# A two-layer hybrid decoder on one core: the weight sums of paired up-projection columns move from VectorE to accumulating transfers that GpSimd issues, and three more pairs of columns are formed

## The chip, the core and the metric

The kernel runs on one core of a Trainium2 chip. The metric is the time of one execution in microseconds, as the device reports it; lower is better. The engines are called as the profile calls them: PE is TensorE, ACT is ScalarE, DVE is VectorE, POOL is GpSimd, SP is SyncE, which here only issues DMAs.

## The reference

The input is 512 tokens of width 1024, with 16 learned tokens put ahead, 528 in all. Each of two layers is a mixer (projections, retention and gated linear attention heads, an output projection) and a gated MLP, each between two RMS norms with a residual. The change touches the MLP's up projection, 1024 to 2 x 2816:

```
def _conv_ffn(h, ffn_up, ffn_conv_w, ffn_conv_b, ffn_down):
    length = h.shape[1]
    u = h @ ffn_up
    up = jnp.pad(u, ((0, 0), (CONV_W - 1, 0), (0, 0)))
    conv = ffn_conv_b + sum(up[:, i:i + length] * ffn_conv_w[i] for i in range(CONV_W))
    a, g = jnp.split(conv, 2, axis=-1)
    return (jax.nn.gelu(a, approximate=True) * g) @ ffn_down
```

Everything is float32 at the kernel's boundary.

## The kernel before, in words

Activations lie transposed: features on the 128 partitions, tokens along the free dimension. Each float32 operand of a large product is split into two float16 parts, a high one and a low one, and a product is three matmuls: high x high, high x low, low x high (lines 534 to 536; in pairs, line 1296). For a weight, ACT makes the high part (a scaled copy) and DVE the low part (scaled weight less the high part). Both go to a buffer called a unit, of which there are 10; PE reads units only.

Weights come in by SP's loads, into float32 stage cells (`st`) of 4 KB per partition: 8 cells in the first layer, 5 in the second. The plan makes one list of blocks for the whole program, and each block is loaded and converted in the order of that list, up to 10 blocks ahead of the one that PE uses. So how far the weights run ahead is set by the cells, by the units, and by how fast ACT and DVE come to them. From the middle of the first mixer on, a scheduler orders the instructions of each engine; loads and, here, some others keep the order of the program.

The up projection has 22 columns per layer. A column here is 128 features of the first half (`upa`) with the 128 features of the gate half that go with them (`upg`). After it come the convolution (ACT one step, DVE two, line 1342), the gelu, the product of the halves and its split into two float16 parts. A plain column is two blocks of 1024 x 128 weights and eight products of 3 matmuls, in two parts by tokens (232 and 296; 218 and 296 in the second layer).

Some columns are instead made as pairs, by a product scheme of the Strassen kind (`paired`, line 1283 on). The weights of the column are a 2 x 2 matrix of quarters, w11, w12 (gate half), w21, w22 (lower 512 rows), and the tokens are cut into two halves of 264. Seven products of 4 x 3 matmuls over 264 tokens take the place of eight. For that, sums of the activations are formed once per layer and sums of the weights for each pair. A pair stands in the list as four pieces (`PairPiece`): piece 0 holds w11 and w22; piece 1 holds w11 + w12 and w12 + w22; piece 2 holds w11 + w12 + w22 and w21; piece 3 holds the sum of all four. Before the change DVE forms the sums in place in two stage cells (line 215), four steps per pair, each between the conversions that read the old value and those that read the new one. PE accumulates the products in PSUM banks (`pp`), from the same three that the plain products use; ACT copies intermediate results out (`part`, line 1304, and `u`, line 1326) and DVE combines them (line 1308).

In the first layer nine columns are pairs: 9, 11, 13, 14, 15, 17, 19, 20, 21; in the second two: 8 and 10. GpSimd takes part in the norms, in rotary steps and in roots, and issues two DMAs late in the program (line 1468).

Of the kernel before, what the change touches and what calls it, by code (L numbers as in the profile page):

```python
# [9 lines left out]
F32 = mybir.dt.float32  # L10
U8 = mybir.dt.uint8
AF = mybir.ActivationFunctionType
ALU = mybir.AluOpType

P = 128
# [30 lines left out]
SLOTS = 41  # L46
AHEAD = 10
# [21 lines left out]
PAIRED = {0: (9, 11, 13, 14, 15, 17, 19, 20, 21), 1: (8, 10)}  # L69
HK2 = KD // 2  # L70
# [117 lines left out]
class PairPiece:  # L188
# [10 lines left out]

    def fetch(self):  # L200
        if self.unit is not None:
            return
        kern, nc = self.kern, self.kern.nc
        if self.step == 0:
            self.st = []
            for half in (((0, 0), (1, 1)), ((0, 1), (1, 0))):
                st = cell(kern.stage, [P, 2, HK2, P], F32, *kern.stage_of(self.layer))
                for i, (a, b) in enumerate(half):
                    load = nc.sync.dma_start(st[:, i], self.src[512 * a : 512 * (a + 1), self.cols[b] : self.cols[b] + P].rearrange("(k p) c -> p k c", p=P))
                    kern.tc.keep_in_program_order(load)  # L210
                self.st += [st[:, 0], st[:, 1]]
                if len(self.st) == 2:
                    self.both = st
        w = self.first.st
        add = lambda to, x: nc.vector.tensor_tensor(out=w[to], in0=w[to], in1=w[x], op=ALU.add)
        if self.step == 0:
            parts = [(slice(0, 2), self.both)]
        elif self.step == 1:
            add(0, 2)
            add(2, 1)  # L220
            parts = [(0, w[0]), (1, w[2])]
        elif self.step == 2:
            add(0, 1)
            parts = [(0, w[0]), (1, w[3])]
        else:
            add(0, 3)
            parts = [(0, w[0])]
        u = self.unit = cell(kern.wpool, [P, 2, 2, HK2, P], F16, "unit", "unit", UNITS)
        for i, st in parts:
            self.hi = nc.scalar.activation(u[:, 0, i], st, AF.Copy, scale=SW)  # L230
            nc.vector.scalar_tensor_tensor(out=u[:, 1, i], in0=st, scalar=SW, in1=u[:, 0, i], op0=ALU.mult, op1=ALU.subtract)


class Kern:
# [495 lines left out]
    def plan(self):  # L730
        a = self.a
# [7 lines left out]
        for l in range(DEPTH):  # L739
# [4 lines left out]
            for i in range(KF):  # L744
                if i in PAIRED[l]:
                    first = None
                    for q in range(4):
                        self.key[l, "pair", i, q] = len(self.blocks)
                        self.blocks.append(PairPiece(self, l, a["ffn_up"][l], (P * i, DFF + P * i), q, first))
                        first = first or self.blocks[-1]  # L750
                    continue
# [889 lines left out]
```

## Time and profile before

| | |
|---|---|
| median of three runs | 1195.14 us (1195.05 to 1195.2) |
| profiled execution, its own time | 1195.35 us |
| its span in the profile | 1193.5 us |
| PE, DVE, ACT, POOL busy | 1183.8, 879.8, 682.5, 184.1 us |
| HBM read | 120.24 MB |
| loads of 256 KB from the up projection's weights (pairs) | 44 |
| loads of 512 KB from the up projection's weights (plain columns) | 66 |

The span is divided into stages, by PE's products: first mixer and output projection to 263 us, first up projection to 495, down projection from 490 to 603, then the second mixer and output projection to 854, the second up projection to 1085, and the last down projection to the end. The pairs of the first layer are used between 362 and 495 us, those of the second between 939 and 974. Busy time on an engine says nothing by itself; what counts is who waits for whom where PE would otherwise go on. In rows of the timeline the columns are start, length, engine, line and operation, output and inputs, and the count of like instructions that follow each other; in rows that group instructions, the busy time, the mean length of one, and the idle time before them with what ended it.

### The profile page before, as it was taken

Reading aid. Unit: us, or ns where it says so; the run is one execution under the profiler, and the core shown is the slowest. Engines: PE = TensorE matmul, PEld = TensorE weight load, DVE = VectorE, ACT = ScalarE, POOL = GpSimd, SP = SyncE. Lnnn points to the kernel's source line nnn. Section 1 sums busy time; section 2 is a strip of 40 time slices with the busy share of each in tenths; the row PEclk is TensorE's granted clock in tenths of the full one; section 3 lists DMA queues with packets and bytes.
Section 4 is the critical chain, followed back from the end, with each engine's and each line's share of the span. In section 5 each row is a group of like instructions: output and inputs, shape, how many; then the busy total and the mean of one; then the engine's idle time right before and its main releaser. Section 6 shows DMA issues by size and latency. Waiting matters only on the chain.

```text
span 1193.5 us, 26242 instructions
## 1 busy us (share of the span) xinstructions
PE 1183.8 (99%) x10910; PEld 998.4 (84%) x10910; DVE 879.8 (74%) x1539; ACT 682.5 (57%) x1351; POOL 184.1 (15%) x213
## 2 busy tenths in 40 slices
PE   8999999999999999999999999999999999999998
PEld 8888889989888888988888888899888888886445
DVE  6687855368998999833565968553799998797687
ACT  6685444564876676633346854445657676664452
POOL 2132311263000000000331414012620000000000
PEclk9999999999999999999999999999999999999999
DMA  8933131122613242642235132211422453206371
GB/s 224 276 108 96 54 90 54 37 65 78 177 36 89 77 119 74 184 112 77 80 99 142 55 89 72 72 54 37 124 71 72 125 164 110 99 1 225 117 250 71
DMA packets 207066, 124.02 MB, mean 104 GB/s; under 512 B 6928, under 2 KB 194500, under 8 KB 206948
## 3 DMA queue, kind: packets, MB, share of 16 engines
q1 hardware_dynamic: 206356, 121.37, 34.8%
q8 instruction: 85, 1.39, 0.5%
q0 software_dynamic: 160, 0.52, 0.1%
q10 hardware_dynamic: 432, 0.46, 0.1%
q14 instruction: 33, 0.27, 0.1%
HBM read 120.24 MB, written 2.10 MB: 103 GB/s over the span
## 4 chain that ended last, share of the span: by engine, by line
PE 87%; DVE 3%; issue 1%; ACT 1%; POOL 1%; POOLq 0%; DVEq 0%; ACTq 0%
PE pu L535 10%; PE pu L534 10%; PE pu L536 10%; PE pl L1480 8%; PE pp L1296 7%; PE pj L534 6%; PE pj L535 6%; PE pj L536 6%; PE pd L534 3%; PE pd L536 3%; PE pd L535 3%; PE po L534 2%; PE po L536 2%; PE po L535 2%; PE o L851 1%
## 5 line engine op out<-in xcount | busy, mean ns | idle before, releaser
L536 PE MATMUL pu<-every,unit 128*128 128x296 f16 (+2 forms) x1056 | 289.1, 274 | 0.0
L535 PE MATMUL pu<-every,unit 128*128 128x296 f16 (+2 forms) x1056 | 289.0, 274 | 0.0
L534 PE MATMUL pu<-every,unit 128*128 128x296 f16 (+2 forms) x1056 | 288.7, 274 | 0.0
L534 PEld LDWEIGHTS <-unit 128*128 128x128 f16 x2508 | 246.1, 98 | 35.4
L536 PEld LDWEIGHTS <-unit 128*128 128x128 f16 x2508 | 245.3, 98 | 36.2
L535 PEld LDWEIGHTS <-unit 128*128 128x128 f16 x2508 | 245.3, 98 | 35.5
L534 PE MATMUL pj<-every,unit 128*128 128x296 f16 (+2 forms) x888 | 244.3, 275 | 0.0
L535 PE MATMUL pj<-every,unit 128*128 128x296 f16 (+2 forms) x888 | 244.3, 275 | 0.0
L536 PE MATMUL pj<-every,unit 128*128 128x296 f16 (+2 forms) x888 | 244.2, 275 | 0.0
L131 DVE SCALAR_TENSOR_TENSOR unit<-st,unit 128x1024 f16<-128x1024 f32 (+2 forms) x161 | 196.7, 1229 | 43.5 <-ACT unit L123 43.3
L123 ACT ACTIVATE unit<-st 128x1024 f16<-128x1024 f32 x159 | 164.9, 1041 | 44.9 <-PE pd L536 20.4
L459 POOL TENSOR_TENSOR every<-every 128x5 f32<-128x5 f32 (+6 forms) x31 | 37.3, 1205 | 556.3 <-DVE every L458 463.2
L1296 PEld LDWEIGHTS <-unit 128*128 128x128 f16 x924 | 90.4, 98 | 14.0 <-issue 0.4
L492 DVE TENSOR_TENSOR acc<-acc,sq 128x296 f32<-128x296 f32 (+2 forms) x60 | 32.3, 541 | 75.0 <-ACT sq L490 69.5
L536 PE MATMUL pd<-av,unit 128*128 128x232 f16 (+1 forms) x308 | 84.7, 276 | 0.0
L535 PE MATMUL pd<-av,unit 128*128 128x232 f16 (+1 forms) x308 | 84.6, 276 | 0.0
L534 PE MATMUL pd<-av,unit 128*128 128x296 f16 (+1 forms) x308 | 84.4, 276 | 0.0
L1353 ACT ACTIVATE u<-pu 128x296 f32<-128x296 f32 (+2 forms) x132 | 49.8, 378 | 49.2 <-PE pu L536 48.0
L1480 PE MATMUL pl<-unit,fk 128*128 128x512 f16 x330 | 71.4, 379 | 0.0
L1342 DVE SCALAR_TENSOR_TENSOR cg<-u,every,cg 128x527 f32<-128x527 f32 (+1 forms) x88 | 66.3, 754 | 4.7 <-ACT cg L1337 4.3
L536 PE MATMUL po<-merged,unit 128*128 128x296 f16 (+2 forms) x256 | 69.7, 274 | 0.0
L535 PE MATMUL po<-merged,unit 128*128 128x296 f16 (+2 forms) x256 | 69.7, 274 | 0.0
(279 smaller groups left out, 1938.9 us busy)
## 6 DMA issues: line engine op xcount, KB each, us to landing
st<-in_ffn_up SPq DMA_DIRECT2D x66, 512.0 KB, 4.8
st<-in_w_in SPq DMA_DIRECT2D x56, 512.0 KB, 4.1
st<-in_ffn_down SPq DMA_DIRECT2D x46, 512.0 KB, 4.9
st<-in_ffn_up SPq DMA_DIRECT2D x44, 256.0 KB, 3.4
st<-in_w_out SPq DMA_DIRECT2D x16, 512.0 KB, 4.1
st<-in_ffn_down SPq DMA_DIRECT2D x8, 384.0 KB, 6.7
out<-yo SPq DMA_DIRECT2D x7, 256.0 KB, 2.0
w<-in_ffn_down SPq DMA_DIRECT2D x3, 512.0 KB, 5.1
```

Source lines behind the costliest of these rows:

```text
L123: self.hi = self.kern.nc.scalar.activation(self.unit[:, 0], self.st, AF.Copy, scale=SW)
L131: self.last = self.kern.nc.vector.scalar_tensor_tensor(out=out, in0=x, scalar=SW, in1=high, op0=ALU.mult, op1=ALU.subtract)
L459: nc.gpsimd.tensor_tensor(out=r[:w, :n], in0=t[:w, :n], in1=self.mhalf[:w, :n], op=ALU.pow)
L492: self.summed = eng.tensor_tensor(out=acc[:, :n], in0=acc[:, :n], in1=sq[:, :n], op=ALU.add)
L534: nc.tensor.matmul(ps[:, :n], w[:, 0, kk, :], x[:, 0, n0:n1], start=first, stop=False)
L535: nc.tensor.matmul(ps[:, :n], w[:, 0, kk, :], x[:, 1, n0:n1], start=False, stop=False)
L536: nc.tensor.matmul(ps[:, :n], w[:, 1, kk, :], x[:, 0, n0:n1], start=False, stop=last)
L851: nc.tensor.matmul(o[:, i, :], intra(i + 1), vn(i + 1), start=i == 0, stop=i == 0, skip_group_check=i > 0)
L1296: mm = lambda p, q, **kw: nc.tensor.matmul(ps, u[:, p, k, :], x[k][:, q], skip_group_check=more, **kw)
L1342: nc.vector.scalar_tensor_tensor(out=to, in0=u[:, max(lo, d) - d : L - d], scalar=self.cvec[:, ci(i) : ci(i) + 1], in1=to, op0=ALU.mult, o ...
L1353: nc.scalar.activation(u[:, n0:n1], ps[:, : n1 - n0], AF.Copy, scale=IXW)
L1480: mm = lambda x, w, **kw: nc.tensor.matmul(ps[:, cols], x, w[:, cols], skip_group_check=more, **kw)
```

## The change

Three things change, all in how pairs are prepared and which columns are pairs.

First, the weight sums are no longer made by DVE. Each pair gets a third cell, with two more quarters: `wa` and `wd`, both loaded as w11. SP now loads six quarters of 256 KB per pair in a given order instead of four. GpSimd then issues five transfers that add what they read to what lies in their destination: with piece 0, w12 from HBM into wa, w22 into w12, w21 into wd, and the new w12 into wd; with piece 1, the new w12 into w11. The first reads HBM, the other four copy inside SBUF. They keep the program's order in GpSimd's queue. Piece 1 is made from wa and w12, piece 2 from w11 and w21, piece 3 from wd. The third cell comes from a ring of four cells of its own in the first layer (`wx`) and from the five stage cells in the second.

Second, piece 0 of each pair changes places in the list with the block ahead of it, so that its loads and sums are asked for one block earlier; the order in which PE uses the blocks is looked up by key and follows.

Third, eleven columns of the first layer are pairs (10, 16 and 18 are new, 15 is plain) and three of the second (12 is new). 

```diff
+WX = 4
-PAIRED = {0: (9, 11, 13, 14, 15, 17, 19, 20, 21), 1: (8, 10)}
+PAIRED = {0: (9, 10, 11, 13, 14, 16, 17, 18, 19, 20, 21), 1: (8, 10, 12)}
...
+    def load(self):
+        kern, nc = self.kern, self.kern.nc
+        more = (kern.keep, "wx", "wx", WX) if self.layer == 0 else (kern.stage, *kern.stage_of(self.layer))
+        cells = [cell(pool, [P, 2, HK2, P], F32, *tag) for pool, *tag in [(kern.stage, *kern.stage_of(self.layer))] * 2 + [more]]
+        quarter = lambda a, b: self.src[512 * a : 512 * (a + 1), self.cols[b] : self.cols[b] + P].rearrange("(k p) c -> p k c", p=P)
+        order = ((0, 0, 0, 0), (0, 1, 1, 1), (1, 0, 0, 1), (2, 0, 0, 0), (1, 1, 1, 0), (2, 1, 0, 0))
+        for c, i, a, b in order:
+            load = nc.sync.dma_start(cells[c][:, i], quarter(a, b))
+            kern.tc.keep_in_program_order(load)
+        (w11, w22), (w12, w21), (wa, wd) = ((c[:, 0], c[:, 1]) for c in cells)
+        self.parts = [(slice(0, 2), cells[0])], [(0, wa), (1, w12)], [(0, w11), (1, w21)], [(0, wd)]
+        self.adds = [(wa, quarter(0, 1)), (w12, w22), (wd, w21), (wd, w12)], [(w11, w12)], [], []
+
+    def sums(self, step):
+        for to, x in self.adds[step]:
+            add = self.kern.nc.gpsimd.dma_start(out=to, in_=x, accum_op=ALU.add)
+            self.kern.tc.keep_in_program_order(add)
...
         if self.step == 0:
...
+            self.load()
+        self.first.sums(self.step)
+        parts = self.first.parts[self.step]
...
-        add = lambda to, x: nc.vector.tensor_tensor(out=w[to], in0=w[to], in1=w[x], op=ALU.add)
-        if self.step == 0:
-            parts = [(slice(0, 2), self.both)]
-        elif self.step == 1:
-            add(0, 2)
-            add(2, 1)
-            parts = [(0, w[0]), (1, w[2])]
-        elif self.step == 2:
-            add(0, 1)
-            parts = [(0, w[0]), (1, w[3])]
-        else:
-            add(0, 3)
-            parts = [(0, w[0])]
...
+                    n = self.key[l, "pair", i, 0]
+                    self.blocks[n - 1 : n + 1] = self.blocks[n - 1 : n + 1][::-1]
+                    self.key = {k: {n - 1: n, n: n - 1}.get(v, v) for k, v in self.key.items()}
```

On POOL, before, the norms of the first layer's second token part (`acc`, the residual in `every`, `tmp`) are followed at once by those of the down projection:

```order
L514 TENSOR_TENSOR every_79<-every_79,tmp_4094 128x296
L514 TENSOR_TENSOR every_79<-every_79,tmp_4100 128x296
L459 TENSOR_TENSOR every_79<-every_79 99x3
L459 TENSOR_TENSOR every_79<-every_79 116x2
L514 TENSOR_TENSOR every_79<-every_79,tmp_8015 128x232
```

After, the sums of all eleven pairs stand between them; here the end of the first norms and the sums of columns 9 and 10 (`st_4288` holds w11 and w22 of column 9, `st_4289` w12 and w21, `wx_4290` wa and wd):

```order
L513 TENSOR_TENSOR every_79<-every_79,tmp_4100 128x296
L458 TENSOR_TENSOR every_79<-every_79 99x3
L216 DMA wx_4290<-in_ffn_up 128x4x128
L216 DMA st_4289<-st_4288 128x512
L216 DMA wx_4290<-st_4289 128x512 x2
L216 DMA st_4288<-st_4289 128x512
L216 DMA wx_4868<-in_ffn_up 128x4x128
L216 DMA st_4867<-st_4866 128x512
L216 DMA wx_4868<-st_4867 128x512 x2
L216 DMA st_4866<-st_4867 128x512
```

In each pair the fifth sum, into the first cell, stands ahead of the next pair's first four.

On ACT, before, the conversions of the pair of column 15 (`st_5684`, `st_5687`) stand among the copies out of PSUM (`part`) of the pairs of columns 13 and 14, `pp_5786` and the two after it, and `pp_5919`:

```order
L1304 ACTIVATE part_5807<-pp_5786 128x264
L230 ACTIVATE unit_5790<-st_5684 128x512
L1393 ACTIVATE ca_5772<-ca_5772 128x528
L1304 ACTIVATE part_5827<-pp_5787 128x264
L230 ACTIVATE unit_5790<-st_5687 128x512
L1304 ACTIVATE part_5845<-pp_5786 128x264
L230 ACTIVATE unit_5810<-st_5687 128x512
L230 ACTIVATE unit_5810<-st_5684 128x512
L463 ACTIVATE av_4523<-cg_5773 128x528
L1304 ACTIVATE part_5938<-pp_5919 128x264
L230 ACTIVATE unit_5830<-st_5684 128x512
```

After, the pair of column 16 is converted there (`st_5718` w11 and w22, `st_5719` w12 and w21, `wx_5720` wa and wd), among the copies of the pairs of columns 13 (`pp_5827`) and 14 (`pp_5970`, `pp_5971`):

```order
L1306 ACTIVATE part_5880<-pp_5827 128x264
L229 ACTIVATE unit_5731<-st_5718 128x1024
L124 ACTIVATE unit_5845<-st_5843 128x1024
L229 ACTIVATE unit_5863<-wx_5720 128x512
L229 ACTIVATE unit_5863<-st_5719 128x512
L229 ACTIVATE unit_5922<-st_5719 128x512
L1306 ACTIVATE part_5984<-pp_5970 128x264
L1306 ACTIVATE part_6001<-pp_5971 128x264
L229 ACTIVATE unit_5922<-st_5718 128x512
L1306 ACTIVATE part_6021<-pp_5970 128x264
L229 ACTIVATE unit_5940<-st_5927 128x1024
```

The conversion of w11 for piece 2 (`unit_5922<-st_5718`) now stands between the copies of the second and the third product of column 14, and reads a value that the sum on POOL must have written since the conversion of `unit_5731`; in the rows of before the sums were DVE's, and wa and wd did not exist.

More of the change, by code (lines that the diff above doesn't have):

```diff
@@ L204, in fetch @@
         if self.step == 0:
[L205 to L215, printed above, removed]
-        if self.step == 0:
-            parts = [(slice(0, 2), self.both)]
-        elif self.step == 1:
-            add(0, 2)
-            add(2, 1)
-            parts = [(0, w[0]), (1, w[2])]
-        elif self.step == 2:
-            add(0, 1)
-            parts = [(0, w[0]), (1, w[3])]
-        else:
-            add(0, 3)
-            parts = [(0, w[0])]
+            self.load()
+        self.first.sums(self.step)
+        parts = self.first.parts[self.step]
         u = self.unit = cell(kern.wpool, [P, 2, 2, HK2, P], F16, "unit", "unit", UNITS)
```

## The prediction

> **What bounds the kernel now.** I read the page first (busy times and the chain that ended last), then the waits of PE, then the two up projections, where the pairs are.
>
> ```profile
> PE 1183.8 (99%) x10910; PEld 998.4 (84%) x10910; DVE 879.8 (74%) x1539; ACT 682.5 (57%) x1351; POOL 184.1 (15%) x213
> ...
> PE 87%; DVE 3%; issue 1%; ACT 1%; POOL 1%; POOLq 0%; DVEq 0%; ACTq 0%
> ```
>
> ```profile
> PE pts L606 <- DVE ndg L714: 1.3, 1, 1.3
> ...
> PE pp L1296 <- ACT part L1304: 0.2, 1, 0.2
> ```
>
> PE is busy for 99% of the span, and its longest waits are 1.3 us in all. In the pairs it waited once, 0.2 us for a copy by ACT. So time is what PE has to stream, plus any stall that is newly made. The stretch of the first up projection with most of its pairs, by engine:
>
> ```profile
> core 0: us, PE busy (x) PEld busy (x) DVE busy (x) ACT busy (x) POOL busy (x), PEclk, DMA share, GB/s
> 362.00:485.00 123.00, 122.80 (x1092) 106.63 (x1090) 115.09 (x177) 85.39 (x153) 0.00 (x0) 1.00 0.37 104
> ```
>
> PE is full at a granted clock of 1.00, DVE is busy 94%, GpSimd not at all, the DMA engines 37%. The waits of this stretch, and DVE's and ACT's groups by form:
>
> ```profile
> ACT unit L230 <- DVE st L215: 12.8, 13, 3.1
> ```
>
> ```profile
> L231 DVE SCALAR_TENSOR_TENSOR unit<-st,unit 128x512 f16<-128x512 f32 x36 | 24.0, 685 | 3.3 <-ACT unit L230 3.1
> L215 DVE TENSOR_TENSOR st<-st 128x512 f32<-128x512 f32 x29 | 19.9, 685 | 0.2
> L131 DVE SCALAR_TENSOR_TENSOR unit<-st,unit 128x1024 f16<-128x1024 f32 x10 | 12.1, 1222 | 1.0 <-ACT unit L123 1.0
> L1308 DVE SCALAR_TENSOR_TENSOR u<-pp,part 128x264 f32<-128x264 f32 x24 | 9.9, 424 | 1.9 <-ACT unit L123 1.1 <-ACT unit L230 0.8
> ...
> L231 DVE SCALAR_TENSOR_TENSOR unit<-st,unit 128x1024 f16<-128x1024 f32 x7 | 8.5, 1216 | 0.0
> ```
>
> ```profile
> L230 ACT ACTIVATE unit<-st 128x512 f16<-128x512 f32 x36 | 21.6, 623 | 13.1 <-DVE st L215 12.3 <-PE pu L536 0.6
> ...
> L1304 ACT ACTIVATE part<-pp 128x264 f32<-128x264 f32 x25 | 9.6, 383 | 8.3 <-PE pp L1296 8.2
> ...
> L230 ACT ACTIVATE unit<-st 128x1024 f16<-128x1024 f32 x7 | 7.3, 1047 | 0.3 <-PE pp L1296 0.3
> ```
>
> ACT already waits for the weight sums on DVE, up to 3.1 us at a time, and PE hardly feels it: units are ready well ahead.
>
> **PE's own saving.** Starts of matmuls that open a column without a pair, in the first and in the second up projection, and pieces of the chain for the pairs:
>
> ```profile
> 340.67 0.26 PE L534 MATMUL pu<-every,unit 128*128 128x232 f16 x1
> ...
> 351.47 0.26 PE L534 MATMUL pu<-every,unit 128*128 128x232 f16 x1
> ```
>
> ```profile
> 907.86 0.26 PE L534 MATMUL pu<-every,unit 128*128 128x218 f16 x1
> ...
> 918.38 0.26 PE L534 MATMUL pu<-every,unit 128*128 128x218 f16 x1
> ```
>
> ```profile
> 374.60 1.35 PE pp L1296 x12
> ...
> 402.93 27.00 PE pp L1296 x240
> ```
>
> A column without a pair costs 351.47 - 340.67 = 10.80 us, in the second projection 918.38 - 907.86 = 10.52. A pair is 7 products of 1.35, 9.45 us (240 matmuls in 27.00 give the same 112.5 ns each). Two more pairs in the first projection and one in the second: 2 x 1.35 + 1.07 = 3.77 us less for PE. Nothing hides this, since PE is the path.
>
> **DVE and ACT.** Removed: 44 sums of 0.685. Added per new pair on DVE: 5 x 0.685 + 1.216 + 3 x 0.424 against 2 x 1.222, so 3.5 us. In the stretch above, 29 sums go (19.9) and two pairs come (7.0): about 102 of 120 us instead of 115 of 123. ACT gains 5 x 0.623 + 1.05 - 2 x 1.05, about 2.1 per pair: 89 of 120. PE did not wait for DVE here, so the relief is worth nothing by itself; it is room for the pairs. What is late next, if anything, are the sums as transfers.
>
> **What the sums cost as transfers.** The trace has no accumulating transfer, so I bound it. Loads of the same 256 KB by SP, and the only transfers that GpSimd issues, also 256 KB, amid a run of SP loads:
>
> ```profile
> L209 SPq DMA_DIRECT2D st<-in_ffn_up x44: 367/498/1904, 301.2 to 922.2; - x44
> ...
> DMA to landing us min/median/max: 2.9/3.4/5.3
> ```
>
> ```profile
> L1468 POOL DMA_DIRECT2D every<-in_post_ffn_norm x2: 554/648/742, 1084.6 to 1085.3; - x2
> ...
> DMA to landing us min/median/max: 6.9/7.2/7.5
> ```
>
> ```profile
> 1082.48 0.37 SPq L153 DMA_DIRECT2D every<-in_ffn_down  x1
> ...
> 1085.24 8.84 SPq L153 DMA_DIRECT2D st<-in_ffn_down  x6
> ```
>
> So a sum takes 2.9 to 7.5 us from issue to landing. By kind it is nearest to the GpSimd row, but that one stood beside a run of SP loads, and the stretch of the pairs moves data only 37% of the time now. I take 5.5, an estimate between the medians 3.4 and 7.2. The fit in the Trainium skill, "DMA: Bandwidth & Descriptors", section "Anatomy of one DMA — SWDGE (gpsimd) path", about 2.0 us plus the bytes at 436 GB/s, would make it 2.6 us (an estimate from that page), and by it no sum would be late; the 6.9 to 7.5 of the trace disagree, and the measurement decides.
>
> Where would lateness reach PE? ACT's rows for pair 16, in the section on the change, are the tightest that I found. From the product whose copy is part_5880 PE makes 7 products of 1.35, 9.45 us, until the bank copied by part_6021 is needed again. Between stand, in a row of dependence: a copy (0.38), the conversion of unit_5731 (1.05), its low part on DVE (1.22), the sum of w12 into w11, its conversion (0.62), the copy part_6021 (0.38). This leaves 9.45 - 3.65 = 5.8 us for the sum. DVE may begin one conv step (about 0.7, as a sum's length) late: 5.5 + 0.7 - 5.8 is 0.4, so I count 0.5 us there. With the lower end, 2.9, it is nothing; with 7.5 it is 2.4. Behind this wait on ACT stand only copies and conversions of the same stretch. The other pairs have as much room or more by the rows, except 13 with 14, where it is about the same.
>
> GpSimd's queue per pair in a run: four issues of 0.65 and one landing, since the second sum into wd waits for two others: 2.6 + 5.5 = 8.1, under 9.45; it reaches 9.45 at 6.85 us a sum. What else GpSimd does here:
>
> ```profile
> 282.49 1.77 POOL L459 TENSOR_TENSOR every<-every 99x3 f32<-99x3 f32 x1 [3.12 <-DVE every L458]
> ```
>
> It is done with the norms before the first pair's loads (below), and next needed in the down projection, so nothing waits behind the sums. SP's queue gets two more loads per pair; they lie behind loads that wait for cells anyway. In the second projection a pair holds three of five cells, and its pairs alternate with plain columns, so five cells turn over per two columns (19.97 us), against a landing of 3.4 and two sums of 5.5: no cost; if that cover is gone, a microsecond late is a microsecond lost. The exchange of piece 0 with the block ahead of it only gives the sums more time: nothing.
>
> **DMA throughput.** Loads with rows of 128 and of 512 columns, when the engines are full:
>
> ```profile
> 436.00:441.00 5.00, 5.00 (x42) 3.90 (x40) 5.00 (x7) 4.82 (x11) 0.00 (x0) 1.00 0.96 262
> ```
>
> ```profile
> 1092.00:1098.00 6.00, 6.00 (x30) 2.71 (x28) 4.79 (x5) 2.00 (x2) 0.00 (x0) 1.00 1.04 400
> ```
>
> 256 KB cost 0.96 us of all engines in short rows (262 over 0.96) and 0.66 in long ones. Per pair: six loads 5.76, the sum from HBM 0.96 to 1.92, four sums inside SBUF 0.66 to 1.31 each (as a plain transfer, or twice that, since a sum reads two sides where a copy reads one). Columns 9 to 21: 11 pairs and 2 x 3.84 give 111 to 150 us, against 11 x 9.45 + 2 x 10.80 = 125.6 on PE. The excess of up to 24 is covered by the lead:
>
> ```profile
> 301.18 2.05 SPq L209 DMA_DIRECT2D st<-in_ffn_up  x4
> ```
>
> ```profile
> 362.27 0.50 PE L1296 MATMUL pp<-every,unit 128*128 128x264 f16 x3
> ```
>
> The first pair's loads leave 61 us before PE uses them; about 20 of it (a landing, two sums, conversions, the queue of units) can't be given up, 41 can. So no cost up to 166 us of transfers, that is up to 1.59 us a sum, 2.4 times a plain one. The gain side is excluded: transfers can make nothing on PE shorter.
>
> **The sum.** The profiled execution took 1195.35 us (span 1193.5 and 1.85 around it), 0.21 over the median of the runs shown. 1195.35 - 3.77 + 0.5 = 1192.1, in terms of the median 1191.9 us. Its own range is 1190.9 (nothing late, the 0.2 us wait and a little of the stalls gone too) to 1192.7.
>
> **The rivals.** *Sums late on ACT.* A sum takes 7.2, as in the GpSimd row. Pair 16 loses 7.2 + 0.7 - 5.8 = 2.1 us, 13 with 14 about as much, and GpSimd's 9.8 per pair passes 9.45 by little in the run of six. 1191.4 + 4.2 is 1195.6; with 6.5 us it is 1194. For it speaks that GpSimd's transfer is the nearest in kind, and DVE near full; against it, that ACT waited 3.1 us for sums and PE did not. No measurable change, chance 0.21.
>
> *Transfers become the bound, and the kernel slower.* It decides from 2.4 times the price of a plain transfer on. At 3 times a sum costs 1.97, the thirteen columns 11 x (5.76 + 2.88 + 7.88) + 7.7 = 189 us, 23 more than are covered: 1191.4 + 23 = 1214; at 2.5 times 3 us are uncovered, 1195. Against it speaks the 0.37 share; for it, that nothing in the trace prices a read of the destination. Chance 0.20 for over 1197.5. The Trainium skill, "Collectives: The Full Stack", section "The bandwidth ceiling: the fold count and why AG ≠ RS ≠ AR", holds that an adding transfer reads two sources for each write and so runs at half the rate of a copy; by it the time would be at the upper end above, 150 us, short of this rival's point. No run here shows it yet.
>
> **How the numbers follow.** The forecast has 0.56, late sums 0.21, slower by transfers 0.20, and 0.03 is for what I don't see, split between same and slower. Within 0.2% (2.4 us) is about what a measurement of this kernel can't tell from no change, so the forecast is faster. The range reaches from 1190.8 through the late sums to 1198.0 and leaves out most of the slower case.
>
> **What would show it.** Right: 36 matmuls fewer on PE, no L215 on DVE, landings of GpSimd's sums near 5.5 us, waits of PE in the pairs under 1 us, 3.8 us less of span. Late sums show as ACT waiting for a DMA at the conversions of st, and PE at pp waiting for ACT. A DMA share near 1 from 320 to 480 and SP's loads landing late show the second rival. I am wrong if PE waits in a stage that the change doesn't touch.

## The result and the profile after

| | before | after |
|---|---|---|
| median | 1195.17 us (1195.05 to 1195.65) | 1209.84 us (1208.92 to 1211.88) |
| profiled execution, its own time | 1195.35 us | 1211.88 us |
| its span | 1193.5 us | 1210.0 us |
| mean granted clock | 1.00 | 0.995 |

The ratio of after to before is 1.0124, with a 95% interval of 1.0111 to 1.0137: the change makes the kernel slower by 1.2%. The forecast was 1191.9 us, faster; the measured time lies 12 us above the end of its range (1198.0), near the 1214 us that the second rival gave for transfers as the bound.

The page of the changed kernel, its busy times, its two large DMA queues (packets, MB, share of 16 engines) and the chain that ended last:

```profile
PE 1186.5 (98%) x10874; PEld 998.4 (83%) x10874; DVE 863.2 (71%) x1516; ACT 686.5 (57%) x1363; POOL 253.0 (21%) x283
...
q1 hardware_dynamic: 221236, 128.72, 36.2%
q0 software_dynamic: 15616, 18.88, 9.8%
...
PE 49%; DVE 7%; issue 2%; DMA 2%; ACT 1%; POOL 0%; POOLq 0%; DVEq 0%; ACTq 0%
```

PE issues 36 matmuls fewer, as the change says, but is busy for longer, and DMA now stands in a chain that was PE for 87%. Queue q0 holds the sums: 18.88 MB of the 148 that the two queues move, but 9.8 points of their 46. The waits of PE, in the whole span, and what ACT and GpSimd waited for between 300 and 520 us:

```profile
PE pp L1298 <- ACT part L1306: 13.5, 7, 4.2
...
PE pp L1298 <- DVE u L1310: 0.9, 1, 0.9
```

```profile
ACT unit L229 <- DMA st<-st: 26.1, 11, 6.3
...
POOL wx L216 <- DMA wx<-st: 21.8, 3, 8.1
```

Before, PE waited 0.2 us in the pairs; now 14.4, nearly all of it for ACT's copies out of PSUM. ACT in turn stood 26.1 us at conversions until a sum inside SBUF had landed. One such wait on ACT, and the stall of PE behind it:

```profile
478.84 0.64 ACT L462 ACTIVATE av<-cg 128x528 f16<-128x528 f32 x1
484.11 1.15 ACT L229 ACTIVATE unit<-st 128x512 f16<-128x512 f32 x2 [4.64 <-DMA st<-st]
...
487.17 0.65 ACT L1306 ACTIVATE part<-pp 128x264 f32<-128x264 f32 x2
```

```profile
481.89 1.51 PE L1298 MATMUL pp<-xs,unit 128*128 128x264 f16 x12
487.59 2.06 PE L1298 MATMUL pp<-xs,unit 128*128 128x264 f16 x12 [4.18 <-ACT part L1306]
```

The copy that PE needs (487.17) waited for nothing of its own; it stands behind the conversion of 484.11 in ACT's fixed order, and that one waited 4.64 us for a sum. The sum had been issued at 476.93, the last row here of GpSimd's timeline (its `x1` rows are single DMA issues, the bracket says what it waited for before):

```profile
441.46 0.87 POOL L216 DMA_DIRECT2D wx<-st  x1 [8.75 <-issue]
442.03 1.18 POOL L216 DMA_DIRECT2D st<-st  x1
...
464.76 0.86 POOL L216 DMA_DIRECT2D wx<-st  x1 [6.10 <-DMA wx<-st]
...
476.39 0.86 POOL L216 DMA_DIRECT2D wx<-st  x1 [6.77 <-issue]
476.93 1.20 POOL L216 DMA_DIRECT2D st<-st  x1
```

From one pair to the next GpSimd takes (476.39 - 441.46) / 3 = 11.6 us, where PE needs 9.45 per pair. In the stretch that was shown of before (362 to 485 us), and in three pieces of the way there:

```profile
362.00:485.00 123.00, 112.36 (x965) 95.68 (x964) 91.67 (x143) 77.24 (x141) 35.85 (x37) 0.97 0.92 194
```

```profile
340.00:360.00 20.00, 20.00 (x181) 17.55 (x180) 17.03 (x25) 12.48 (x24) 4.84 (x5) 1.00 0.82 164
360.00:380.00 20.00, 19.84 (x175) 16.87 (x174) 14.15 (x22) 14.03 (x26) 0.88 (x1) 1.00 0.60 145
...
420.00:440.00 20.00, 20.00 (x180) 17.39 (x179) 13.64 (x21) 12.49 (x23) 4.89 (x5) 1.00 1.15 237
```

The DMA share went from 0.37 to 0.92, and DVE from 115 busy microseconds to 92: the relief of DVE came (though a part of these 23 us is only that the stretch got less done), and is worth nothing, as forecast. PE lost 10.4 us of busy time in this stretch.

The stalls cost more than their length. The windows behind the three long ones show it in the clock column (the eighth, ahead of DMA share and GB/s):

```profile
409.00:413.00 4.00, 3.87 (x21) 2.81 (x21) 3.14 (x5) 2.18 (x6) 0.00 (x0) 0.61 0.48 135
...
445.00:449.00 4.00, 3.91 (x24) 2.77 (x23) 2.46 (x5) 1.34 (x3) 1.33 (x2) 0.70 1.23 216
...
488.00:492.00 4.00, 4.00 (x23) 2.79 (x22) 2.49 (x4) 0.92 (x2) 0.00 (x0) 0.57 0.45 133
```

PE runs at half clock for up to 3.4 us after each of these stalls. At 112.5 ns per matmul, the 36, 24 and 24 matmuls behind them lost about 1.7, 1.3 and 1.7 us, 4.6 in all (in the second case a part of the half clock fell into the stall itself). So the account is: 14.4 us of waits; 0.16 us more at each of the eight stalls, since the row of a product is 1.51 us long where its cost is 1.35, so 1.3 in all; 4.6 of half clock; less the 3.8 saved. That is the 16.5 us by which the spans differ.

### The profile page after: what moved, and what is told of

Same layout as the page of the kernel before. It is cut to its first block, busy times and chain, and to the rows that moved or that the text cites. A ratio compares the mean times of both kernels' runs of the same rounds, so it can differ in the third digit from the quotient of the medians.

```text
span 1210.0 us, 26430 instructions
## 1 busy us (share of the span) xinstructions
PE 1186.5 (98%) x10874; PEld 998.4 (83%) x10874; DVE 863.2 (71%) x1516; ACT 686.5 (57%) x1363; POOL 253.0 (21%) x283
## 3 DMA queue, kind: packets, MB, share of 16 engines
q0 software_dynamic: 15616, 18.88, 9.8%
q8 instruction: 85, 1.39, 0.5%
## 4 chain that ended last, share of the span: by engine, by line
PE 49%; DVE 7%; issue 2%; DMA 2%; ACT 1%; POOL 0%; POOLq 0%; DVEq 0%; ACTq 0%
PE pl L1482 8%; PE pj L533 4%; PE pj L534 4%; PE pj L535 4%; PE pu L534 3%; PE pu L533 3%; PE pu L535 3%; PE pd L534 3%; PE pd L535 3%; PE pd L533 3%; PE pp L1298 3%; PE po L533 1%; PE po L534 1%; PE po L535 1%; DMA st<-in_ffn_up 1%
## 5 line engine op out<-in xcount | busy, mean ns | idle before, releaser
L535 PE MATMUL pu<-every,unit 128*128 128x296 f16 (+2 forms) x960 | 262.8, 274 | 0.0
L534 PE MATMUL pu<-every,unit 128*128 128x296 f16 (+2 forms) x960 | 262.6, 274 | 0.0
L533 PE MATMUL pu<-every,unit 128*128 128x296 f16 (+2 forms) x960 | 262.4, 274 | 0.0
L132 DVE SCALAR_TENSOR_TENSOR unit<-st,unit 128x1024 f16<-128x1024 f32 (+1 forms) x155 | 189.9, 1231 | 52.3 <-ACT unit L124 52.0
L124 ACT ACTIVATE unit<-st 128x1024 f16<-128x1024 f32 (+1 forms) x153 | 158.8, 1042 | 60.8 <-PE pd L535 22.2
L1298 PE MATMUL pp<-xs,unit 128*128 128x264 f16 x672 | 84.8, 283 | 13.6 <-ACT part L1306 13.5
L1344 DVE SCALAR_TENSOR_TENSOR ca<-u,every,ca 128x512 f32<-128x512 f32 (+2 forms) x88 | 66.6, 758 | 6.1 <-ACT ca L1339 5.6
L535 PE MATMUL po<-merged,unit 128*128 128x296 f16 (+2 forms) x256 | 69.7, 274 | 0.0
```

Source lines behind the costliest of these rows:

```text
L124: self.hi = self.kern.nc.scalar.activation(self.unit[:, 0], self.st, AF.Copy, scale=SW)
L132: self.last = self.kern.nc.vector.scalar_tensor_tensor(out=out, in0=x, scalar=SW, in1=high, op0=ALU.mult, op1=ALU.subtract)
L533: nc.tensor.matmul(ps[:, :n], w[:, 0, kk, :], x[:, 0, n0:n1], start=first, stop=False)
L534: nc.tensor.matmul(ps[:, :n], w[:, 0, kk, :], x[:, 1, n0:n1], start=False, stop=False)
L535: nc.tensor.matmul(ps[:, :n], w[:, 1, kk, :], x[:, 0, n0:n1], start=False, stop=last)
L1298: mm = lambda p, q, **kw: nc.tensor.matmul(ps, u[:, p, k, :], x[k][:, q], skip_group_check=more, **kw)
```

## The experiments

Two theories stood at the start. *Waiting*: each sum is a little late, and the fixed orders of ACT and of GpSimd's queue turn that into stalls of PE. *Traffic* (the price of a sum): an adding transfer takes so much more of the DMA engines than a plain one that eleven pairs in thirteen columns ask for more than the engines can move, and everything lands late. All times below are medians beside runs of the kernel before of 1195.2 to 1195.4 us on the same chip; the interval is that of the ratio to it.

| kernel | us | ratio to before | DMA share 362 to 485 | landing of a sum, median us |
|---|---|---|---|---|
| the change | 1209.8 | 1.0111 to 1.0137 | 0.92 | 6.5 |
| no sums | 1191.9 | 0.9960 to 0.9982 | 0.47 | |
| the pairs of the change, sums on DVE | 1201.8 | 1.0038 to 1.0068 | 0.30 | |
| the change with the pairs of before | 1197.4 | 1.0007 to 1.0026 | 0.87 | 6.6 |
| sums that nobody reads | 1202.9 | 1.0037 to 1.0070 | 0.92 | 6.7 |
| sums over half of the elements | 1196.5 | 1.0003 to 1.0021 | 0.73 | 4.2 |
| three sums by transfers, two on DVE | 1244.5 | 1.0397 to 1.0433 | 0.68 | 6.3 |
| the same without DVE's sum into wd | 1194.7 | 0.9986 to 1.0005 | 0.75 | 6.4 |
| two sums by transfers, two on DVE | 1191.7 | 0.9959 to 0.9982 | 0.64 | 5.8 |
| that form with the pairs of before | 1195.7 | 0.9994 to 1.0013 | 0.55 | 6.5 |
| all sums by GpSimd's additions | 1232.8 | 1.0299 to 1.0334 | 0.28 | |
| plain copies in place of sums | 1193.9 | 0.9979 to 0.9998 | 0.71 | 4.5 |
| five sums, no wait in GpSimd's queue | 1206.5 | 1.0077 to 1.0110 | 0.95 | 7.2 |

**No sums.** The change with its lists of sums empty:

```diff
-        self.adds = [(wa, quarter(0, 1)), (w12, w22), (wd, w21), (wd, w12)], [(w11, w12)], [], []
+        self.adds = [], [], [], []
```

> The changed kernel with its 11 and 3 pairs, six loads per pair and exchanged piece 0, but the sums are left out: nothing is added to the quarters, so 70 transfers of GpSimd and their waits are gone. Waiting theory (ACT, in its fixed order, waits for late sums and holds up the copies that PE needs) and traffic theory (the sums cost the DMA engines more than twice a plain transfer, so that everything lands late) both expect no stall of PE in the pairs and 1191.4 to 1192.5 us. If it stays above 1195, it is the six loads, the exchange or the pairs themselves that cost, and both theories are wrong.

Measured 1191.89 us, with no wait of PE in the pairs over 0.2 us:

```profile
PE pp L1298 <- ACT part L1306: 0.3, 2, 0.2
```

So PE's saving is as computed (1191.4), and six loads per pair, the exchange of piece 0 and the pairs cost nothing that shows. The whole loss, 1209.84 - 1191.89 = 18.0 us, is the sums'.

**The pairs alone.** The kernel before with the new set of pairs:

```diff
-PAIRED = {0: (9, 11, 13, 14, 15, 17, 19, 20, 21), 1: (8, 10)}
+PAIRED = {0: (9, 10, 11, 13, 14, 16, 17, 18, 19, 20, 21), 1: (8, 10, 12)}
```

> The kernel before, sums on DVE, with the 11 and 3 pairs of the change: the pairs alone. DVE then has about 115 + 2 x 6.2 = 127 us of work for the 120 us of the stretch, so it falls behind by some 7 us, which the units made ahead can partly cover. Both theories: PE saves 3.77 and loses 0 to 7, 1191.5 to 1198 us. If it is 1210 as with the change, the pairs and not the transfers are the cause.

Measured 1201.75 us, 4 us over the upper end. DVE is full, and at the end PE stalls:

```profile
362.00:485.00 123.00, 120.79 (x1068) 104.16 (x1067) 119.87 (x193) 83.85 (x154) 0.00 (x0) 1.00 0.30 85
```

```profile
PE pp L1296 <- ACT part L1304: 4.8, 1, 4.8
```

DVE is busy 119.87 of 123 us, and the stall of 4.8 us (after two of about 1 us) drags a half clock behind it, which my expectation did not hold. So on DVE there is no room for eleven pairs: taking work off DVE is needed for them, though it was worth nothing for nine.

**The pairs of before, sums by transfers.** The change with the set of pairs of before (the line taken out in the last diff).

> The change with the columns of before: nine pairs and two, sums by transfers. Waiting theory: pairs stand at most three in a row, GpSimd's queue (11 to 12 us per pair against 9.45 on PE) catches up in each plain column between, but a single late sum can still hold up ACT: one or two stalls of 3 to 4 us with the half clock behind each, 1196 to 1203 us. Traffic theory: 9 x 13.5 + 4 x 3.84 = 137 us of transfers against 128 on PE, an excess that the lead covers, 1195 to 1196 us.

Measured 1197.42 us, 2 us over before, with stalls of 0.8 us and less and one of 1.1 in the second projection, and no half clock. It lies in the range of the waiting theory. The traffic theory let the lead cover the excess and expected 1196 us at most, so the lead covers less than it took it to; the DMA share of the stretch is 0.87, just under full. The sums cost 2 us here and 18 with two pairs more: the loss grows steeply where the engines fill up.

**Sums that nobody reads.** In the first layer the sums go into cells of the third ring, of this and of the pair before, and the pieces are made from the loaded quarters:

```diff
+            self.parts = [(slice(0, 2), cells[0])], [(0, w22), (1, w12)], [(0, w11), (1, w21)], [(0, w22)]
+            va, vd = kern.last_wx or (wa, wd)
+            self.adds = [(wa, quarter(0, 1)), (wd, w22), (va, w21), (wd, w12)], [(vd, w12)], [], []
+            kern.last_wx = wa, wd
```

> The change, but in the first layer the sums go into cells of the third ring that nothing reads, and the pieces are made from the loaded quarters: the same bytes, four sums inside SBUF and one from HBM per pair, in the same queue at about the same times, without any conversion that waits for a sum (the part left out is the sums' use). Waiting theory: the stalls of PE are gone, 1191.5 to 1193.5 us. Traffic theory: loads land as late as with the change, ACT waits for them, 1203 to 1210 us.

Measured 1202.85 us, between the two. The waits of ACT say why this does not decide:

```profile
ACT cg L1345 <- DMA wx<-st: 11.8, 1, 11.8
...
ACT part L1312 <- DMA wx<-st: 4.5, 1, 4.5
```

No conversion waited for a sum or for a load. But a conv step and a copy waited for sums. My reading, which the trace does not show, is that they write to memory that a cell of the third ring had held, and which counted as free since nothing read it. The two stalls of PE (5.6 and 2.3 us, each with its half clock) come behind these two waits. So full traffic alone did not make a load too late for ACT, but the time is that of another wait, and the run is inconclusive.

**Half of the elements.**

```diff
-            add = self.kern.nc.gpsimd.dma_start(out=to, in_=x, accum_op=ALU.add)
+            add = self.kern.nc.gpsimd.dma_start(out=to[:, :2], in_=x[:, :2], accum_op=ALU.add)
```

> The change with each sum over the first half of its elements only (128 KB instead of 256; the other half of each destination stays as loaded): as many transfers, the same waits, half the bytes. If a sum's length is set by its bytes (at about 1.7 us of all DMA engines per 256 KB, so 13.5 us of transfers per pair against 9.45 on PE, now 9.7), sums land in 4 to 4.5 us, GpSimd's cycle per pair falls under 9.45 and PE's stalls go: 1191.9 to 1195 us. If it is set by a fixed latency and by waiting in order, landings stay at 6 us and the time at 1203 to 1210.

Measured 1196.54 us; sums land in 4.2 us (median), the DMA share falls to 0.73. Half the bytes take away 13.3 of the 18.0 us. What is left is mainly one stall of 2.55 us and its half clock, behind a conversion on ACT that waited 6.9 us for a sum inside SBUF.

**Three sums by transfers, two on DVE.** The sums into wa, w12 and wd (from w21) stay transfers; DVE adds w12 into w11 and into wd:

```diff
+        self.adds = [(wa, quarter(0, 1)), (w12, w22), (wd, w21)], [], [], []
+        self.late = [], [], [(w11, w12)], [(wd, w12)]
...
+        for to, x in self.late[step]:
+            self.kern.nc.vector.tensor_tensor(out=to, in0=to, in1=x, op=ALU.add)
```

> The change with three sums per pair by transfers (w12 into wa, w22 into w12, w21 into wd, none of which waits for another) and two on DVE (w12 into w11, w12 into wd), so GpSimd's queue holds no wait for a landing of its own any more. Waiting theory, in the form that GpSimd's cycle of 11 to 12.3 us per pair is what falls behind: the cycle is gone, 1191.5 to 1194 us. Traffic theory: 5.8 + 2.1 + 2 x 1.45 = 10.8 us per pair, 15 us over PE's time in eleven pairs, inside the lead if that can be used, 1192 to 1196; stalls of PE for late sums of w22 into w12 would remain.

Measured 1244.52 us, far worse than anything expected. The waits of DVE and PE:

```profile
DVE wx L220 <- DMA wx<-st: 41.3, 11, 6.2
...
PE pp L1301 <- ACT part L1309: 26.3, 3, 17.4
```

In each of the eleven pairs DVE came to its addition into wd while the transfer of w21 into wd was still under way, and stood up to 6.2 us with everything else of its queue behind it. Of all waits for transfers in these runs, this one on DVE cost most. A later run without that addition tests this:

```diff
-        self.late = [], [], [(w11, w12)], [(wd, w12)]
+        self.late = [], [], [(w11, w12)], []
```

> The kernel with three sums by transfers, without DVE's addition of w12 into wd (left out, so piece 3 is not the sum of all four); the transfers are the same. Theory of order: DVE stood 41.3 us in that addition, waiting for the landing of w21 into wd, and everything behind it on DVE was late; without it the time falls from 1244.5 to 1192 to 1197 us. Theory of traffic: 10.8 us of transfers per pair are the cause, and it stays over 1215.

Measured 1194.70 us: 50 us come back with one addition of 0.69 us per pair, while the transfers stay. So the place of the wait was the cause there, not the traffic; nor was it the work of the addition, since the next kernel has two additions per pair on DVE as well. Sums still land in 6.4 us here, as late as in the change, and do little harm (1194.70 against 1191.89 us without sums): what counts is who stands and waits.

**Two sums by transfers, two on DVE, five loads.** wd isn't needed, since DVE forms the sum of all four in w21:

```diff
+        self.parts = [(slice(0, 2), cells[0])], [(0, wa), (1, w12)], [(0, w11), (1, w21)], [(0, w21)]
+        self.adds = [(wa, quarter(0, 1)), (w12, w22)], [], [], []
+        self.late = [], [], [(w11, w12)], [(w21, w11)]
```

> The change with two sums per pair by transfers (w12 into wa, w22 into w12), two on DVE (w12 into w11, the new w11 into w21) and five loads instead of six, since wd is not needed. Both theories: 5 x 0.96 + 2.1 + 1.45 = 8.35 us of transfers per pair, under the 9.45 of PE, no wait inside GpSimd's queue, DVE has half of the sums it had before: 1191.5 to 1194 us. Should it be the best form, it lies below the kernel before and close to the one without sums (1191.9).

Measured 1191.74 us, a ratio to before of 0.9971 (0.9959 to 0.9982): faster than both kernels, and as fast as without any sum.

```profile
362.00:485.00 123.00, 122.39 (x1083) 105.71 (x1081) 114.94 (x181) 89.91 (x162) 15.55 (x14) 1.00 0.64 154
```

PE is as full as before, with eleven pairs; DVE is at 115 us, as before, DMA at 0.64. To see whether the form or the pairs bring this, the same form with the pairs of before:

> The form with two sums by transfers and two on DVE, with the nine and two pairs of before. If that form only allows more pairs and is worth nothing by itself, as the waits of PE before (0.2 us in the pairs) say: 1195.0 to 1195.6 us. If relieving DVE is worth something by itself: 1194.5 or less. If the sums still cost where PE can't hide them: over 1196.

Measured 1195.72 us, ratio 0.9994 to 1.0013, 0.1 us over the band that I gave for no effect: the form is worth nothing by itself, it only makes room for the pairs.

**All sums by GpSimd's additions.** The kernel before with the new pairs and its sums on GpSimd:

```diff
-        add = lambda to, x: nc.vector.tensor_tensor(out=w[to], in0=w[to], in1=w[x], op=ALU.add)
+        add = lambda to, x: kern.tc.keep_in_program_order(nc.gpsimd.tensor_tensor(out=w[to], in0=w[to], in1=w[x], op=ALU.add))
```

> The kernel before with the 11 and 3 pairs, its four sums per pair made by GpSimd's own additions instead of DVE's, no transfers. From a 128x296 addition of 1.1 us on GpSimd a 128x512 one is about 1.9 (an estimate), 7.6 us per pair, under 9.45; each sum is 1.2 us slower than on DVE in a chain that ACT waits for four times per pair. Waiting theory: stalls at the tight pairs only, 1193 to 1200 us. Traffic theory has nothing to add here: 1191.5 to 1193.

Measured 1232.76 us; both expectations missed. The groups of GpSimd and of DVE in the stretch, by form:

```profile
L215 POOL TENSOR_TENSOR st<-st 128x512 f32<-128x512 f32 x30 | 49.2, 1639 | 76.4 <-DVE unit L231 75.7
```

```profile
L231 DVE SCALAR_TENSOR_TENSOR unit<-st,unit 128x512 f16<-128x512 f32 x35 | 30.3, 886 | 6.4 <-ACT unit L230 5.8
L1342 DVE SCALAR_TENSOR_TENSOR cg<-u,every,cg 128x527 f32<-128x527 f32 x11 | 15.4, 1399 | 0.0
```

An addition takes 1.64 us on GpSimd, less than the 1.9 estimated, but DVE's own instructions became longer beside it: a low part 886 ns where it took 685, a conv step 1399 where the changed kernel has 765 for the same form. The work taken off DVE came back as longer work on DVE. The Trainium skill, "SBUF — State Buffer", section "Who interferes with whom", says that a DVE instruction with two inputs in SBUF contends with a GpSimd instruction that reads SBUF. The trace agrees: between 300 and 520 us the 36 low parts of 128x512 without an addition of GpSimd beside them took 681 ns in the mean, and the 19 with one took 1163 and up to 1759, while the combining steps of L1308, which have one of their two inputs in PSUM, took 421 both ways.

**The price by itself.** No decoder: 256 KB transfers by GpSimd alone on the chip, each kind first singly, then eight at once, then adding ones beside loads by SP. The core of it:

```diff
+    for i in range(4):
+        keep(g.dma_start(out=cells[i], in_=cells[i + 12], accum_op=ALU.add))
+        gate(cells[i : i + 1])
...
+    for i in range(8):
+        keep(g.dma_start(out=cells[i], in_=cells[i + 12], accum_op=ALU.add))
+    gate(cells[:8])
```

> No decoder at all (the output is a copy of x): 256 KB transfers by GpSimd, in the shapes of the change, on engines with nothing else to do. First one at a time, four of each kind: a plain copy inside SBUF, an adding one, a plain load from HBM, an adding one from HBM; then eight of each kind at once; then eight adding ones beside twelve loads by SP. Price theory: one alone lands in 3 to 4.5 us also when it adds, eight at once take 0.7 us each as plain copies and 1.4 to 1.7 when they add, and beside the loads of SP they land at 6 us or more. Latency theory: an adding transfer alone takes 6 us already, and eight at once are little slower than plain ones.

Singly, from issue to landing: a plain copy inside SBUF (L111) and an adding one (L114):

```profile
L111 POOL DMA_DIRECT2D room<-room x4: 539/550/707, 25.2 to 33.0; - x4
...
DMA to landing us min/median/max: 2.2/2.3/2.4
```

```profile
L114 POOL DMA_DIRECT2D room<-room x4: 832/844/881, 35.6 to 46.3; - x4
...
DMA to landing us min/median/max: 3.2/3.3/3.3
```

A plain load from HBM took 3.3 us in the same way, an adding one 4.5. When eight are in flight, GpSimd's small copies that wait for one landing after the other show the price of each: two rows of plain copies, two of adding ones, two of adding ones from HBM:

```profile
90.74 0.18 POOL L102 COPY mark<-room 128x1 f32<-128x1 f32 x1 [0.48 <-DMA room<-room]
91.38 0.18 POOL L102 COPY mark<-room 128x1 f32<-128x1 f32 x1 [0.46 <-DMA room<-room]
...
103.20 0.18 POOL L102 COPY mark<-room 128x1 f32<-128x1 f32 x1 [1.20 <-DMA room<-room]
104.59 0.19 POOL L102 COPY mark<-room 128x1 f32<-128x1 f32 x1 [1.21 <-DMA room<-room]
...
132.59 0.19 POOL L102 COPY mark<-room 128x1 f32<-128x1 f32 x1 [1.39 <-DMA room<-in_ffn_up]
134.36 0.18 POOL L102 COPY mark<-room 128x1 f32<-128x1 f32 x1 [1.58 <-DMA room<-in_ffn_up]
```

That is 0.64 us per plain copy, 1.39 per adding one, 2.2 times as much, and 1.77 per adding one from HBM. The last figure is less sure, since GpSimd issued these 1.5 to 2.0 us apart and it may be the pace of the issues. The queue of the sums in the changed kernel agrees with such prices: it took 9.8% of 1210 us for 72 transfers (two of them no sums), 1.65 us each. Beside twelve loads by SP the adding ones landed after 5.2 to 14.3 us, 10.7 in the median. The price theory has it right: alone a sum is quick, in company it is slow. With these prices and the prediction's 0.96 per load a pair takes 5.76 + 1.77 + 4 x 1.39 = 13.1 us of all engines, against 9.45 on PE.

**Plain copies in place of sums.**

```diff
-            add = self.kern.nc.gpsimd.dma_start(out=to, in_=x, accum_op=ALU.add)
+            add = self.kern.nc.gpsimd.dma_start(out=to, in_=x)
```

> The change with its five transfers per pair as plain copies that overwrite their destination instead of adding to it (the sums are what is left out): as many transfers, the same bytes, the same queue and the same waits. Price theory (an adding transfer takes over twice the engines' time): landings fall to 3.5 to 4.5 us, GpSimd's cycle per pair under 9.45, 1191.9 to 1195 us. Latency theory (any transfer that GpSimd issues lands late, and waiting in order does the rest): landings of about 6 us and 1203 to 1210 us.

Measured 1193.92 us; landings 4.5 us in the median, stalls of 1.2 us at most, no half clock. The queue of GpSimd on the page:

```profile
q0 software_dynamic: 5760, 18.88, 4.7%
```

The same 18.88 MB, but 5760 packets instead of 15616, and 4.7% of the engines' span instead of 9.8. Only the adding is taken out, and 1209.84 - 1193.92 = 15.9 us of the 18.0 go with it (GpSimd's issues are shorter for plain copies as well, 0.54 us against 0.85 and more).

**Five sums without GpSimd's wait in its queue.** So far each kernel that mended the loss had fewer bytes to move and also a shorter wait in GpSimd's queue. This one keeps five adding transfers and their readers, and takes only that wait away:

```diff
+        self.parts[3][0] = (0, w22)
+        self.adds = [(wa, quarter(0, 1)), (w12, w11), (wd, w21)], [(w22, w21), (w11, w21)], [], []
```

> The change with as many sums of the same bytes (per pair one from HBM, four inside SBUF), but none that waits for the landing of another: w12 into wa, w11 into w12 and w21 into wd with piece 0, w21 into w22 and w21 into w11 with piece 1; piece 3 is made from w22 (other sums than the scheme's, so that only the waits are the same as in the change: each piece still reads what a sum wrote). Queue theory (GpSimd's own wait for a landing in each pair makes its cycle 11 to 12.3 us, and that falls behind PE): the cycle falls to about 5 us of issues, stalls go, 1192 to 1196 us. Theory of bytes (five sums at twice the price and six loads are 13.2 us of all DMA engines per pair against 9.45 on PE, whatever the queue does): landings grow to 8 us and more, ACT waits for them as before, 1203 to 1212 us.

Measured 1206.53 us. GpSimd waited for a landing of its own once, 0.9 us; its sums landed in 7.2 us (the theory of bytes had expected 8 and more), and it and ACT waited like this:

```profile
POOL st L217 <- DVE unit L231: 99.7, 9, 20.7
...
ACT unit L230 <- DMA st<-st: 22.0, 9, 3.5
```

```profile
362.00:485.00 123.00, 111.88 (x967) 95.17 (x965) 96.14 (x150) 80.12 (x147) 35.85 (x37) 0.98 0.95 198
```

The engines are as full as with the change, sums land later, and the loss stays (3.3 us of it went, over 14 stayed). GpSimd still waited 99.7 us for DVE, since the sums with piece 1 overwrite what DVE has to read first. But a sum that is issued after such a wait still takes its landing: the last two were issued at 474.60 us, ACT's conversion could start at 482.06 after 3.24 us of waiting, and PE stood 2.94 us behind it. GpSimd's wait for a landing of its own was thus a place where lateness showed, and not its main source. The main source is the bytes at the price of adding: the run with plain copies moves as many bytes, and is only 2 us above the one without sums.

## Why the prediction was wrong

**PE's saving** of 3.77 us was right: without sums the kernel takes 1191.89 us, and 1195.35 - 3.77 - 0.2 is 1191.4.

**DVE's relief is worth nothing by itself**: right (the mixed form with the old pairs, ratio 0.9994 to 1.0013). That it is room for the pairs was right as well, and more so than I saw: on DVE the eleven pairs cost 1201.75.

**The step that failed is "The excess of up to 24 is covered by the lead".** The amount was about right: adding costs 2.2 times a plain copy inside SBUF, 1.39 us against my upper bound of 1.31, and 1.77 from HBM against 1.92. By the prices of transfers by themselves, 11 x 13.1 + 7.7 = 152 us of transfers stand against 125.6 of PE, 26 too much. But the 41 us of lead couldn't be spent on it, though the prediction itself had the loads of SP "behind loads that wait for cells". SP's queue, at the loads of the up projection:

```profile
333.83 0.63 SPq L105 DMA_DIRECT2D st<-in_ffn_up  x1
350.36 1.47 SPq L208 DMA_DIRECT2D st<-in_ffn_up  x3
...
353.15 0.51 SPq L208 DMA_DIRECT2D wx<-in_ffn_up  x1
369.42 0.37 SPq L105 DMA_DIRECT2D st<-in_ffn_up  x1
```

By 334 us the cells were full; SP then stood from 334 to 350 and from 353 to 369 until cells came free, and the DMA share fell to 0.60 between 360 and 380 while most of the pairs were still to come. A lead is only worth what the buffers hold. In the run of six pairs at the end (from 436 us on) nothing of it was left: at GpSimd's pace they are 6 x (11.6 - 9.45) = 13 us too slow, and lost were waits of 4.11, 0.87, 0.90 and 4.18 us, 0.16 more at each, and half clocks of 1.3 and 1.7, 13.7 us. That the two figures are close is no proof, since the 11.6 us are themselves drawn out by late landings. No run here has more cells, so how much of the loss a lead that could be used would have taken stays open. The point from which the second rival decides, put at 2.4 times the plain price, was too high; the rival's mechanism is what happened, at 2.2 times. The Trainium skill, "Collectives: The Full Stack", section "The bandwidth ceiling: the fold count and why AG ≠ RS ≠ AR", has the adding transfers of a collective at half the rate of copies, since they read two sources; the runs agree for transfers within one core (9.8% against 4.7%, 1.39 against 0.64 us). I took it as the upper end and trusted the lead.

**A sum of 5.5 us** was too short a term, and the wrong kind of term. It is 3.3 us alone, 6.5 in the median here, 11.5 at most, and 10.7 beside SP's loads: a landing time taken at a DMA share of 0.37 does not hold at 0.92. The fit in the Trainium skill, "DMA: Bandwidth & Descriptors", section "Anatomy of one DMA — SWDGE (gpsimd) path", 2.6 us by my estimate from it, is near the 2.3 of a plain copy alone, and below every sum of 256 KB that was measured.

**GpSimd's queue, 8.1 us per pair**: 11.6 measured. The form (issues and one landing) was right. But in the last four pairs 8.6 to 11.3 us passed from the issue of the first sum into wd to that of the second, and GpSimd stood idle for 6.1 to 8.8 of them, where I had counted 5.5. That it is the main cause was refuted by the last run.

**The room at pair 16**, where I counted 0.5 us: its conversion of w11 (at 419.80 us) waited 1.67 us for the sum, and PE did not stall there. The long stalls came at other pairs, as lateness added up. That ACT's wait would hold up the copies behind it, the first rival, was right as the way by which a late sum reaches PE; its size was not, 4.2 us in all against 14.4, and no half clock.

**The second projection, no cost**: 1.2 us of stalls (at 963 and 982 us) in three pairs; wrong by that much. The first rival's second part, GpSimd past 9.45 us per pair, was right.

**What would show it** named the right signs: ACT waiting for a DMA at the conversions, a DMA share near 1 from 320 to 480. The loads of 256 KB landed later as well, in 5.0 us (median) instead of 3.4, but without any sums they took 4.9: that sign says nothing.

Not settled: how the 18 us divide between late sums and the stretched waits of ACT, DVE and GpSimd for each other, which all follow from the full engines; and the kernel with unread sums, whose stalls have another cause.

## What to carry to other kernels

A transfer that adds took about twice the DMA engines' time of a copy here: sum up all transfers of the densest stretch at that price, and compare with the pace at which buffers come free there, not with the lead at its start. What can be moved off a full engine need not all be moved: two of the sums as transfers and two left on DVE made the kernel 3.6 us faster, five made it 15 us slower. Where an engine with a fixed order reads what a transfer writes, ask what stands behind that instruction; the same late landing cost nothing in one place and 50 us in another.

## What the hardware showed that I had not expected

A stall of PE of little more than 2 us can also lower its clock. Four stalls of PE, with the idle time ahead in brackets: in the kernel with all sums by GpSimd's additions, in the one with sums that nobody reads, in the one with sums over half of the elements, and again in the first of these:

```profile
455.65 2.86 PE L1296 MATMUL pp<-xs,unit 128*128 128x264 f16 x24 [1.87 <-ACT part L1304]
```

```profile
473.16 2.80 PE L1304 MATMUL pp<-xs,unit 128*128 128x264 f16 x12 [2.33 <-ACT part L1312]
```

```profile
438.94 5.31 PE L1298 MATMUL pp<-xs,unit 128*128 128x264 f16 x31 [2.55 <-ACT part L1306]
```

```profile
514.48 2.86 PE L1296 MATMUL pp<-xs,unit 128*128 128x264 f16 x24 [3.36 <-ACT part L1304]
```

After 1.87 us idle 24 matmuls took 2.86 us, the full rate; after 2.33 us twelve took 2.80, half of it, and after 2.55 us 31 took 5.31. But the length of the stall alone does not decide: after 3.36 us 24 matmuls took 2.86 us, the full rate again. The traces keep a record of the granted clock, in which the clock changes only at times that are multiples of 3.41 us apart. If the time between 20 and 1170 us of every run of the decoder is cut into these steps, the clock fell from full to half after each of the 19 steps in which PE was idle for 2.03 us or more, and after none with 1.90 us or less. The stall of 3.36 us lay across two steps, with 1.55 us in one and 1.81 in the other. In the changed kernel the three falls added 1.7, 1.3 and 1.7 us to the stalls. The Trainium skill, "TensorE: Matmul & The Clock Gate", section "What's actually happening", gives about 3.4 us for both, the idle time that brings the clock down and the busy time that brings it back. The 3.4 us of half clock agree; the idleness that was enough here is shorter, 2.03 us within one step.

Transfers that add inside SBUF cost 2.2 times a copy, and GpSimd takes 0.84 us to issue one where a plain one takes 0.55.
